# Building the gate table of a product-key retrieval: VectorE's key numbers in PSUM, and half of the second one-hots on VectorE

## The chip, the cores and the metric

The kernel runs on one core of one Trainium2 chip. The metric is device time in microseconds, from one launch that takes all inputs and gives all outputs. The kernel before takes 2154.51 us (median of three runs, 2152.59 to 2160.33). Engines are named as the profile names them: PE is TensorE (PEld its weight loads), DVE is VectorE, ACT is ScalarE, POOL is GpSimd, SP is SyncE, which here only issues DMAs.

## The reference, cut to what matters

One transformer layer on 512 tokens of 1024 channels: a token mixer (dilated and differential attention, gated, projected), then a retrieval over 128 x 128 = 16384 experts of one neuron each, then a last norm. The change touches only the retrieval of the second 256 tokens.

```
# per token and head: 16 best of 128 x 128 product keys, softmax over them
ids   = key1 * 128 + key2              # 8 heads x 16 slots = 128 experts per token
gates = softmax(best_s)
u = u_tab[ids];  act = gelu(einsum('cd,chkd->chk', x, u))
v = v_tab[ids];  out = einsum('chkd,chk->cd', v, gates * act)
```

For a token, the gates can be written as a 128 x 128 table G with G[key2, key1] = sum over the token's 128 slots of gate * (key2 of the slot) one-hot * (key1 of the slot) one-hot. That is a matrix product of two one-hot matrices, with slots as the summed dimension, and it is how the kernel gets the table for the second 256 tokens.

## The kernel before, in words

The tokens go through in two halves of 256. The first half's retrieval is done by rows: for each of its tokens' slots a row of `u_tab`, later of `v_tab`, is gathered (indirect DMA, line 814, issued by POOL) and multiplied or added on DVE (lines 842 and 852); 56 of the `v_tab` rows of one tile are added on PE instead (line 871, with a diagonal matrix that ACT makes in line 868). These rows are "pumped": a few are issued with each piece of the other work, by a table of rates (`RATE`; per four tokens of the gate table 0.45 rows of line 842 and 0.4 of line 871). The places of gathered rows, of raw weights and of those diagonal matrices are one ring of seven.

The second half's retrieval goes over all experts: 64 passes with the whole of `u_tab` and `v_tab` (lines 1102 to 1155, called the sweep below), weighted by the gate table. The gate table is built before the sweep, in a loop over 64 groups of four tokens (line 1157). A group is called a slot of the loop below. One slot is:

- o2, the one-hots of key 2 of four tokens (128 x 512): `iota` holds the key numbers 0 to 127 along the columns, `idT[:, 1]` the chosen keys, a token a column. In every fourth slot (`O3 = 4`) DVE makes it with one comparison (line 1162); in the other 48 slots POOL subtracts (line 1164), and ACT makes a one-hot of the difference with a square and a relu of one minus it (lines 1165 and 1166).
- o1, the one-hots of key 1 times the gates: four comparisons on DVE, one a token, with key and gate as per-partition scalars (line 1168).
- four products on PE into one PSUM bank (line 1172; two bank tiles `s_ps` in turn), and two copies of the bank into the table by ACT (lines 1174 and 1175).
- the pumped rows, issued after the slot's last product.

`iota`, `idT`, o1 and o2 all lie in SBUF. o1 and o2 of a slot are the two halves of one tile `one`; there are four such tiles, two for even and two for odd slots, so a slot's one-hots can't be written before the products of the slot four earlier are done. Before the loop, `idT` is turned round by six transposes on PE (line 1117), each copied back by ACT (line 1118).

The order of the work on each engine is made by the compiler layer's list scheduler from the program order, priorities and its own durations, and each engine works off its list in order. Semaphores carry the dependencies between engines.

Of the kernel before, what the change touches and what calls it, by code (L numbers as in the profile page):

```python
# [11 lines left out]
F32 = mybir.dt.float32  # L12
# [5 lines left out]
ALU = mybir.AluOpType  # L18
# [4 lines left out]
P = 128  # L23
# [13 lines left out]
# rows of the retrieval issued with each weight unit, block or slot of the other work, by stage  # L37
# [17 lines left out]
O3 = 4  # L55
# [30 lines left out]
def block(ctx, tc, x, cT, w_ada, bT, b_row, g1T, norm2_g, w_in, w_pa, w_pb, w_out, lq1, lk1, lq2, lk2,  # L86
# [18 lines left out]
    def shared(nm):  # L105
        """the places of weights and of gathered rows, in turn"""
        return wp.tile([P, D], F32, name=nm, tag="wraw", bufs=7)
# [3 lines left out]
    def place_of(kind, nm, dt=F32):  # L111
        """a unit among the weights' places: raw, high and low parts; a third of the parts only in the front"""
# [8 lines left out]
    def front_place(i):  # L121
        """sixteen units of the front, none of which waits for another's place"""
# [24 lines left out]
    def rsqrt(v, n, nm):  # L147
        """1/sqrt(v), [P, n]"""
# [23 lines left out]
    # ---- small operands  # L172
# [18 lines left out]
    # ---- silu(c)  # L191
# [5 lines left out]
    # ---- modulation: sums over the eight rows of a partition, then over the partitions  # L197
# [24 lines left out]
    def first_modulation(i):  # L222
        """shift and scale of the channels 256 i .. 256 i + 256"""
# [22 lines left out]
    def mod_rows(sec, t):  # L246
        """sections 2..5 of the modulation, a row each in DRAM; the second scale with its norm's weights"""
# [25 lines left out]
    # ---- first norm  # L273
# [63 lines left out]
    # ---- weights in two parts that the one-pass product carries exactly  # L337
    def load_unit(src, nm):
        """src: a [P, a, b] view of DRAM with a b = 1024"""
# [14 lines left out]
    def cols(src, kt, c0, nm):  # L354
        """128 columns, for use as the stationary side"""
# [11 lines left out]
    def cols256(src, kt, c0, nm):  # L367
        """256 columns, for use as the moving side"""
# [4 lines left out]
    def mm3(out_ps, a, b, kt, last=0):  # L373
        """sum over k of a.T @ b, both in two parts; last: the side whose low part is used last"""
# [10 lines left out]
    # ---- relative position bias, as bands  # L385
# [20 lines left out]
    def bias_band(t, h, at, o, m, w):  # L406
        """t[p, at + i w + j] = vec[head, o + i LEN_D + p + j], i < m: rows of a block in reverse"""
# [4 lines left out]
    # ---- lambda  # L412
# [16 lines left out]
    # queries by head: head s of a pair keeps its half of the rows, the other half is zero. The queries of a block  # L429
    # stand in reverse, as the bands do; the transpose of the outputs turns them back.  # L430
# [12 lines left out]
    # ---- keys and values of the first half wait in DRAM for the second  # L443
# [3 lines left out]
    def query(hin, c0, q, nm):  # L447
        """q: [P, 2, HW]"""
# [8 lines left out]
    def key(b, hin, c0, k, i):  # L457
        """k: [P, T]"""
# [24 lines left out]
    # ---- dilated attention: the three groups of a head share one softmax, which is what their merge by  # L483
    # denominators amounts to
# [61 lines left out]
    # ---- differential attention  # L546
    def diff_block(n, q, kk, bd, vb, po, at):
        """one block of queries: q [P, 2, P], keys, bias band, values by block"""
# [23 lines left out]
    def diff_finish(ob, dst, h0):  # L572
        """norm of two heads' outputs, ob: [P, 2, HW], transposed and split into dst"""
# [21 lines left out]
    def mixer(b, between):  # L595
        """attention of half b: both branches' outputs in two parts, channels on partitions"""
# [49 lines left out]
    # ---- the retrieval's choice  # L646
# [8 lines left out]
    def begin_topk(n, t):  # L655
        """t: [P, 768]"""
# [14 lines left out]
    # a pair of ranks (i, j) can be among the best sixteen only if (i + 1)(j + 1) <= 16: row 0 whole, eight of  # L671
    # rows 1..7, one of rows 8..15, in the order of the full table
# [4 lines left out]
    def choose(n, h0, nh, out):  # L677
        """row and column keys of the chosen pairs, heads h0 .. h0 + nh: two [P, 16 nh], a slot a column"""
# [32 lines left out]
        # the keys at those ranks: one of sixteen, small integers that bfloat16 holds exactly  # L711
# [22 lines left out]
    def scores(n, h, qts, held=None):  # L734
        """two tiles, one head: qts: both halves of the queries, [P, HW]"""
# [323 lines left out]

    _, held = tail(0, oa, ob, finish, retrieve)  # L1060

    # ---- second half
    idT = sb.tile([P, 3, 256], F32, name="idT")

    def choose_late(b, g):
# [165 lines left out]
```

## Time and profile before

| what | value |
|---|---|
| median of three runs | 2154.51 us |
| lowest, highest run | 2152.59, 2160.33 us |
| span of the profiled execution | 2148.4 us |
| median of the runs less that span | 6.1 us |
| PE, DVE busy | 1875.4 us (87%), 1839.9 us (86%) |
| POOL, ACT busy | 1257.4 us (59%), 970.7 us (45%) |
| stage of the gate table on DVE | 1209.63 to 1370.28 us |

The profile gives one execution, of which it records the span from the first to the last instruction; what lies around the span is taken as the difference to the median, 6.1 us. Busy time is the union of an engine's records; a record's duration reaches from its start to its end, and on DVE the next record can begin a little (some 0.08 us) before the last one ends, so the pitch from start to start of back-to-back instructions is shorter than the duration. A tuple such as 328/335/3780 is smallest, median and largest duration in ns.

### The profile page before, as it was taken

Reading aid. Unit: us, or ns where it says so; the run is one execution under the profiler, and the core shown is the slowest. Engines: PE = TensorE matmul, PEld = TensorE weight load, DVE = VectorE, ACT = ScalarE, POOL = GpSimd, SP = SyncE. Lnnn points to the kernel's source line nnn. Section 1 sums busy time; section 2 is a strip of 40 time slices with the busy share of each in tenths; the row PEclk is TensorE's granted clock in tenths of the full one; section 3 lists DMA queues with packets and bytes.
Section 4 is the critical chain, followed back from the end, with each engine's and each line's share of the span. In section 5 each row is a group of like instructions: output and inputs, shape, how many; then the busy total and the mean of one; then the engine's idle time right before and its main releaser. Section 6 shows DMA issues by size and latency. Waiting matters only on the chain.

```text
span 2148.4 us, 34562 instructions
## 1 busy us (share of the span) xinstructions
PE 1875.4 (87%) x12324; PEld 1668.1 (78%) x12324; DVE 1839.9 (86%) x3515; ACT 970.7 (45%) x1725; POOL 1257.4 (59%) x797
## 2 busy tenths in 40 slices
PE   6999989887778799878687877889999999999995
PEld 6889889887666687768684455678988889998885
DVE  7757865689999999899889999978999898888777
ACT  2544575442333356543232366534444444444442
POOL 2323323456676676667675766667675665655564
PEclk9999999999999999989798999999999999999998
DMA  9968766758898999889956755788888999998886
GB/s 296 281 198 255 212 178 178 233 175 265 281 313 280 315 325 315 295 291 307 304 186 228 251 169 184 247 284 309 316 316 313 343 346 324 342 335 309 306 308 236
DMA packets 369889, 588.00 MB, mean 274 GB/s; under 512 B 24962, under 2 KB 261002, under 8 KB 369716
## 3 DMA queue, kind: packets, MB, share of 16 engines
q1 hardware_dynamic: 295700, 316.79, 45.3%
q0 software_dynamic: 73728, 268.47, 35.6%
q8 instruction: 97, 1.59, 0.3%
q14 instruction: 76, 0.62, 0.1%
q10 hardware_dynamic: 288, 0.52, 0.1%
HBM read 575.13 MB, written 10.58 MB: 273 GB/s over the span
## 4 chain that ended last, share of the span: by engine, by line
PE 37%; DVE 35%; DMA 14%; issue 8%; POOL 3%; ACT 2%; SPq 1%; POOLq 0%; DVEq 0%; ACTq 0%
PE mm L379 12%; PE acc L1154 9%; PE s_ps L379 9%; DVE grow L842 8%; DMA grow<-in_v_tab_dram,ids 7%; DVE one L1168 3%; DVE wacc L210 2%; DMA wa<-in_w_ada_dram 2%; POOL grow L814 1%; DVE elo L291 1%; DMA grow<-in_u_tab_dram,ids 1%; PE s_ps L1172 1%; DVE rep L666 1%; PE sc L509 1%; DVE acc_rows L852 1%
## 5 line engine op out<-in xcount | busy, mean ns | idle before, releaser
L814 POOL DMA_INDIRECT grow<-in_v_tab_dram,ids x256 | 331.8, 1296 | 300.8 <-DVE ga L852 59.0
L814 POOL DMA_INDIRECT grow<-in_u_tab_dram,ids x256 | 329.6, 1287 | 221.7 <-DVE grow L842 69.8
L842 DVE SCALAR_TENSOR_TENSOR grow<-grow,h 128x1024 f32<-128x1024 f32 x256 | 350.7, 1378 | 6.9 <-DMA grow<-in_u_tab_dram,ids 5.4
L290 ACT CAST ehi<-eraw 128x1024 fp32r<-128x1024 f32 x145 | 152.6, 1053 | 228.7 <-PE acc L1154 75.7
L852 DVE SCALAR_TENSOR_TENSOR ga<-grow,act,ga 128x1024 f32<-128x1024 f32 x127 | 162.8, 1282 | 58.2 <-DMA grow<-in_v_tab_dram,ids 57.6
L290 ACT CAST more<-eraw 128x1024 fp32r<-128x1024 f32 x111 | 116.7, 1051 | 152.7 <-PE acc L1154 62.1
L379 PEld LDWEIGHTS s_ps<-h2T,more 128*128 128x128 f32 x1320 | 166.5, 191 | 4.9 <-ACT more L290 0.2
L1154 PE MATMUL acc<-more,w 128*128 128x512 f32 x672 | 163.4, 392 | 7.3 <-DVE w L291 6.4
L379 PE MATMUL s_ps<-h2T,more 128*128 128x256 f32 x1320 | 168.2, 283 | 0.0
L1154 PE MATMUL acc<-ehi,w 128*128 128x512 f32 x576 | 151.3, 399 | 17.4 <-DVE w L291 14.8
L852 DVE SCALAR_TENSOR_TENSOR acc_rows<-grow,act,acc_rows 128x1024 f32<-128x1024 f32 x71 | 124.4, 1751 | 38.7 <-DMA grow<-in_v_tab_dram,ids 38.2
L1154 PEld LDWEIGHTS acc<-more,w 128*128 128x128 f32 x672 | 127.1, 189 | 34.7 <-DVE w L291 6.8
L379 PE MATMUL s_ps<-h2T,ehi 128*128 128x256 f32 x1168 | 152.0, 283 | 0.0
L379 PEld LDWEIGHTS s_ps<-h2T,ehi 128*128 128x128 f32 x1168 | 145.8, 192 | 0.6
L291 DVE TENSOR_TENSOR elo<-eraw,ehi 128x1024 fp32r<-128x1024 f32 x95 | 136.0, 1432 | 9.4 <-ACT ehi L290 9.2
L1154 PEld LDWEIGHTS acc<-ehi,w 128*128 128x128 f32 x576 | 103.7, 190 | 42.6 <-DVE w L291 21.6
L291 POOL TENSOR_TENSOR elo<-eraw,ehi 128x1024 fp32r<-128x1024 f32 x50 | 123.0, 2459 | 12.6 <-ACT ehi L290 11.8
L1168 DVE TENSOR_SCALAR one<-iota,idT 128x128 f32<-128x128 f32 x256 | 116.5, 534 | 0.3 <-ACT idT L1118 0.3
L379 PE MATMUL mm<-wh_v,h 128*128 128x256 f32 x640 | 102.0, 311 | 15.5 <-ACT wh_v L290 13.1
L1172 PEld LDWEIGHTS s_ps<-one 128*128 128x128 f32 x512 | 69.2, 203 | 54.4 <-ACT G L1175 22.2
L291 DVE TENSOR_TENSOR more<-eraw,more 128x1024 fp32r<-128x1024 f32 x75 | 103.7, 1384 | 6.7 <-ACT more L290 6.5
L871 PE MATMUL ga<-grow,diag 128*128 128x512 f32 x224 | 108.1, 627 | 0.1
(304 smaller groups left out, 4682.5 us busy)
## 6 DMA issues: line engine op xcount, KB each, us to landing
eraw<-in_uT_dram SPq DMA_DIRECT2D x128, 512.0 KB
eraw<-in_v_tab_dram SPq DMA_DIRECT2D x128, 512.0 KB
wa<-in_w_ada_dram SPq DMA_DIRECT2D x48, 512.0 KB
w_v<-in_w_in_dram SPq DMA_DIRECT2D x40, 512.0 KB
w_k<-in_w_in_dram SPq DMA_DIRECT2D x40, 512.0 KB
w_gl<-in_w_in_dram SPq DMA_DIRECT2D x32, 512.0 KB
w_wql<-in_w_q_dram SPq DMA_DIRECT2D x32, 512.0 KB
w_q<-in_w_in_dram SPq DMA_DIRECT2D x24, 512.0 KB
```

Source lines behind the costliest of these rows:

```text
L210: nc.vector.scalar_tensor_tensor(acc, wa[:, k, :], c, acc, op0=ALU.mult, op1=ALU.add)
L290: nc.scalar.copy(hi, src)
L291: (eng or nc.vector).tensor_sub(lo, src, hi.bitcast(F32))
L379: r = nc.tensor.matmul(out_ps, a(i, k), b(j, k), start=(n == 0), stop=(n == 3 * kt - 1))
L509: nc.tensor.matmul(pS[:, at[g] - o:at[g] - o + w[g]], q[g][:, s, n * P:(n + 1) * P], k3[g][:, first[g] * P:(gn + 1) * P], start=True, stop ...
L814: nc.gpsimd.indirect_dma_start(out=r, out_offset=None, in_=tab, in_offset=bass.IndirectOffsetOnAxis(ap=ids[:, s:s + 1], axis=0))
L842: nc.vector.scalar_tensor_tensor(r, r, 1.0, h2, op0=ALU.mult, op1=ALU.mult, accum_out=a)
L852: nc.vector.scalar_tensor_tensor(acc[n], r, a, acc[n], op0=ALU.mult, op1=ALU.add)
L871: nc.tensor.matmul(pe_acc[0][:, sl], dg, r[:, sl], start=(s == 0), stop=(s == NPE - 1), skip_group_check=True)
L1154: nc.tensor.matmul(acc[b][hf], w[i][:, 256 * j + P * b:256 * j + P * b + P], V[jj][:, hf, :], start=(e == 0 and i + jj == 0), stop=(e == N ...
L1168: nc.vector.tensor_scalar(o1[:, t, :], iota, idT[:, 0, t0 + t:t0 + t + 1], idT[:, 2, t0 + t:t0 + t + 1], op0=ALU.is_equal, op1=ALU.mult)
L1172: last = nc.tensor.matmul(pg[:, t * P:(t + 1) * P], o2[:, t, :], o1[:, t, :], start=True, stop=True)
```

## The change

VectorE's comparisons of the table's loop read the key numbers from a PSUM bank. A new pool `pg` holds this bank (`iota_ps`, filled once by ACT before the loop) and three bank tiles `g_ps` for the loop's products, in place of the two tiles that the products shared with the sweep. `O3` goes from 4 to 2, so that DVE makes o2 in every second slot (32 of 64), and POOL and ACT in the others. POOL still reads `iota` from SBUF. The sweep's pool `pp` with `s_ps` and the four accumulators is opened after the loop, when `pg` is given back. The rest of the diff takes out comments and is left out here.

```
-O3 = 4
+O3 = 2
...
-    pp = ctx.enter_context(tc.tile_pool(name="pp", bufs=1, space=PSUM))
+    pg_guard = tc.tile_pool(name="pg", bufs=1, space=PSUM)
+    pg = pg_guard.__enter__()
+
+    def g_ps():
+        return pg.tile([P, 512], F32, name="g_ps", tag="g", bufs=3)
...
-    acc = [[pp.tile([P, 512], F32, name=f"acc{b}{hf}") for hf in range(2)] for b in range(2)]
...
+    iota_ps = pg.tile([P, 512], F32, name="iota_ps")[:, 0:P]
+    nc.scalar.copy(iota_ps, iota)
     for t0 in range(0, 256, 4):
...
-        pair2 = (iota[:, None, :].to_broadcast([P, 4, P]), idT[:, 1, t0:t0 + 4][:, :, None].to_broadcast([P, 4, P]))
+        along = [P, 4, P]
+        key2 = idT[:, 1, t0:t0 + 4][:, :, None].to_broadcast(along)
         if t0 // 4 % O3 == 0:
-            nc.vector.tensor_tensor(o2, *pair2, ALU.is_equal)
+            nc.vector.tensor_tensor(o2, iota_ps[:, None, :].to_broadcast(along), key2, ALU.is_equal)
         else:
-            nc.gpsimd.tensor_tensor(o2, *pair2, ALU.subtract)
+            nc.gpsimd.tensor_tensor(o2, iota[:, None, :].to_broadcast(along), key2, ALU.subtract)
...
-            nc.vector.tensor_scalar(o1[:, t, :], iota, idT[:, 0, t0 + t:t0 + t + 1],
+            nc.vector.tensor_scalar(o1[:, t, :], iota_ps, idT[:, 0, t0 + t:t0 + t + 1],
...
-        pg = s_ps()
+        pt = g_ps()
...
+    pg_guard.__exit__(None, None, None)
+    pp = ctx.enter_context(tc.tile_pool(name="pp", bufs=1, space=PSUM))
+    acc = [[pp.tile([P, 512], F32, name=f"acc{b}{hf}") for hf in range(2)] for b in range(2)]
```

In the changed kernel the comparison for o2 is line 1167, POOL's subtraction 1169, ACT's two activations 1170 and 1171, the comparisons for o1 line 1173, the fill of the bank line 1160, the products 1177 and their copies 1179 and 1180.

How the work stands on DVE at the start of the loop, before (`oh` is scratch of the choice of the last keys, `idT` the chosen keys, `grow` a gathered row):

```order
L719 TENSOR_TENSOR oh<-oh 128x128x8
L1162 TENSOR_TENSOR one<-iota,idT 128x512
L719 TENSOR_TENSOR oh<-oh 128x128x4
L719 TENSOR_TENSOR oh<-oh 128x128x2
L722 TENSOR_TENSOR idT<-oh 128x64 x2
L842 SCALAR_TENSOR_TENSOR grow,act_9338<-grow,h_1_9336 128x1024
L1168 TENSOR_SCALAR one<-iota,idT 128x128 x16
L842 SCALAR_TENSOR_TENSOR grow,act_9338<-grow,h_1_9336 128x1024
L1162 TENSOR_TENSOR one<-iota,idT 128x512
L1168 TENSOR_SCALAR one<-iota,idT 128x128 x8
```

And with the change, at the same place of DVE's list:

```order
L719 TENSOR_TENSOR oh<-oh 128x128x8
L719 TENSOR_TENSOR oh<-oh 128x128x4
L719 TENSOR_TENSOR oh<-oh 128x128x2
L722 TENSOR_TENSOR idT<-oh 128x64 x2
L842 SCALAR_TENSOR_TENSOR grow,act_9338<-grow,h_1_9336 128x1024 x2
L1167 TENSOR_TENSOR one<-iota_ps,idT 128x512
L1173 TENSOR_SCALAR one<-iota_ps,idT 128x128 x8
L1167 TENSOR_TENSOR one<-iota_ps,idT 128x512
L1173 TENSOR_SCALAR one<-iota_ps,idT 128x128 x8
L842 SCALAR_TENSOR_TENSOR grow,act_9338<-grow,h_1_9336 128x1024
```

The first comparison for o2 no longer stands inside the choice of the last keys; two row products stand ahead of the first one-hots, and after that there is one comparison for o2 with every eight for o1.

On ACT at the same place, before (`diag` are the diagonal matrices of line 868, `tp` the bank of the transposes):

```order
L1118 COPY idT<-tp 128x128 x2
L1165 ACTIVATE one<-one 128x512
L1166 ACTIVATE one<-one 128x512
L1165 ACTIVATE one<-one 128x512
L868 ACTIVATE diag<-ident,act_5631 128x128 x8
L1166 ACTIVATE one<-one 128x512
L1165 ACTIVATE one<-one 128x512
L1118 COPY idT<-tp 128x128
L1166 ACTIVATE one<-one 128x512
L1118 COPY idT<-tp 128x128 x3
L1174 COPY G_12228<-s_ps 128x16x4
```

And with the change:

```order
L1118 COPY idT<-tp 128x128 x2
L1170 ACTIVATE one<-one 128x512
L1171 ACTIVATE one<-one 128x512
L1170 ACTIVATE one<-one 128x512
L868 ACTIVATE diag<-ident,act_5631 128x128 x8
L1171 ACTIVATE one<-one 128x512
L1118 COPY idT<-tp 128x128 x4
L1160 COPY iota_ps<-iota 128x128
L1179 COPY G_12228<-g_ps 128x16x4
```

The fill of `iota_ps` (line 1160) stands behind all six copies of `idT`, and two activations of one slot are gone from in front of them.

On POOL, from the first slot on, before:

```order
L814 DMA grow<-in_u_tab_dram,ids_3662 128x1024
L1164 TENSOR_TENSOR one<-iota,idT 128x512 x3
L814 DMA grow<-in_v_tab_dram,ids_3661 128x1024
L814 DMA grow<-in_u_tab_dram,ids_3662 128x1024
L814 DMA grow<-in_v_tab_dram,ids_3661 128x1024
L814 DMA grow<-in_u_tab_dram,ids_3662 128x1024
L814 DMA grow<-in_v_tab_dram,ids_3661 128x1024
L1164 TENSOR_TENSOR one<-iota,idT 128x512 x2
```

And with the change:

```order
L814 DMA grow<-in_u_tab_dram,ids_3662 128x1024
L1169 TENSOR_TENSOR one<-iota,idT 128x512 x2
L814 DMA grow<-in_v_tab_dram,ids_3661 128x1024
L814 DMA grow<-in_u_tab_dram,ids_3662 128x1024
L814 DMA grow<-in_v_tab_dram,ids_3661 128x1024
L814 DMA grow<-in_u_tab_dram,ids_3662 128x1024
L814 DMA grow<-in_v_tab_dram,ids_3661 128x1024
L814 DMA grow<-in_u_tab_dram,ids_3662 128x1024
L1169 TENSOR_TENSOR one<-iota,idT 128x512
```

The gathers are the same; of POOL's runs of two and three subtractions, mostly single ones are left.

## Rows read from the trace of the kernel before

**Rows 1.** The page's first line.

```profile
span 2148.4 us, 34562 instructions
```

**Rows 2.** Busy time by window, for the loop's stage; the first row names the columns.

```profile
core 0: us, PE busy (x) PEld busy (x) DVE busy (x) ACT busy (x) POOL busy (x), PEclk, DMA share, GB/s
1209.63:1370.28 160.65, 122.00 (x604) 85.53 (x603) 160.20 (x334) 101.13 (x249) 110.39 (x102) 0.92 0.58 187
```

**Rows 3.** Groups by line in this window: count, busy us, mean ns, idle before.

```profile
L1168 DVE TENSOR_SCALAR one<-iota,idT 128x128 f32<-128x128 f32 x256 | 116.5, 534 | 0.3 <-ACT idT L1118 0.3
...
L1164 POOL TENSOR_TENSOR one<-iota,idT 128x512 f32<-128x512 f32 x48 | 51.5, 1091 | 8.3 <-PE s_ps L1172 6.2 <-ACT diag L868 1.5
L842 DVE SCALAR_TENSOR_TENSOR grow<-grow,h 128x1024 f32<-128x1024 f32 x28 | 33.7, 1212 | 0.0
...
L814 POOL DMA_INDIRECT grow<-in_u_tab_dram,ids x28 | 31.5, 1127 | 23.4 <-DVE grow L842 10.7 <-DVE one L1168 9.1 <-PE s_ps L1172 1.7
L1165 ACT ACTIVATE one<-one 128x512 f32<-128x512 f32 x48 | 29.8, 628 | 35.7 <-POOL one L1164 35.7
...
L1162 DVE TENSOR_TENSOR one<-iota,idT 128x512 f32<-128x512 f32 x16 | 14.8, 924 | 0.0
```

**Rows 4.** Timeline, 1231 to 1239 us: start, duration, instructions merged.

```profile
1231.12 4.55 DVE L1168 TENSOR_SCALAR one<-iota,idT 128x128 f32<-128x128 f32 x4
...
1232.04 3.03 POOL L1164 TENSOR_TENSOR one<-iota,idT 128x512 f32<-128x512 f32 x3
...
1236.74 2.14 DVE L1168 TENSOR_SCALAR one<-iota,idT 128x128 f32<-128x128 f32 x8
```

**Rows 5.** Timeline at the start of the loop, 1209 to 1219 us.

```profile
1209.63 3.78 DVE L1162 TENSOR_TENSOR one<-iota,idT 128x512 f32<-128x512 f32 x1
...
1209.82 3.04 POOL L1164 TENSOR_TENSOR one<-iota,idT 128x512 f32<-128x512 f32 x3
...
1216.00 0.24 ACT L1118 COPY idT<-tp 128x128 f32<-128x128 f32 x1
...
1216.28 4.28 DVE L1168 TENSOR_SCALAR one<-iota,idT 128x128 f32<-128x128 f32 x16 [0.33 <-ACT idT L1118]
...
1218.46 0.27 ACT L1118 COPY idT<-tp 128x128 f32<-128x128 f32 x1 [0.56 <-PE tp L1117]
```

**Rows 6.** Single lines on DVE: count, smallest/median/largest ns, first and last start.

```profile
L1168 DVE TENSOR_SCALAR one<-iota,idT x256: 328/335/3780, 1216.3 to 1370.0; 128x128 f32<-128x128 f32 x128
...
L1162 DVE TENSOR_TENSOR one<-iota,idT x16: 676/678/3779, 1209.6 to 1362.3; 128x512 f32<-128x512 f32 x16
...
L979 DVE TENSOR_SCALAR h_k<-tp,m2T x8: 531/542/547, 432.5 to 1080.3; 128x256 f32<-128x256 f32 x8
...
L954 DVE TENSOR_TENSOR ot<-mm,mod x16: 408/416/425, 404.6 to 1060.8; 128x256 f32<-128x256 f32 x16
...
L955 DVE TENSOR_TENSOR x<-x,ot x16: 408/458/3037, 408.5 to 1062.4; 128x256 f32<-128x256 f32 x16
...
L791 DVE TENSOR_TENSOR grow<-grow,acc x4: 671/680/680, 2132.1 to 2136.6; 128x512 f32<-128x512 f32 x4
```

**Rows 7.** Timeline of the second norm's transposes, in both halves: reads from PSUM.

```profile
434.97 0.54 DVE L979 TENSOR_SCALAR h_k<-tp,m2T 128x256 f32<-128x256 f32 x1
435.43 0.53 DVE L979 TENSOR_SCALAR h_k<-sc,m2T 128x256 f32<-128x256 f32 x1
...
1074.38 0.73 POOL L980 TENSOR_TENSOR h2T<-h_k,h2T 128x256 fp32r<-128x256 f32 x1 [1.49 <-DVE h_k L979]
...
1074.61 0.55 DVE L979 TENSOR_SCALAR h_k<-sc,m2T 128x256 f32<-128x256 f32 x1 [0.31 <-ACT h2T L978]
```

**Rows 8.** Timeline of PE in the loop, 1227 to 1231 us.

```profile
1227.00 1.88 PE L871 MATMUL ga<-grow,diag 128*128 128x512 f32 x4
...
1228.71 1.95 PE L1172 MATMUL s_ps<-one 128*128 128x128 f32 x16
```

**Rows 9.** The page's group of row sums in the sweep, and what ended DVE's idle time before them.

```profile
L852 DVE SCALAR_TENSOR_TENSOR ga<-grow,act,ga 128x1024 f32<-128x1024 f32 x127 | 162.8, 1282 | 58.2 <-DMA grow<-in_v_tab_dram,ids 57.6
```

More of the change, by code (lines that the diff above doesn't have):

```diff
@@ L1167, in block @@
         for t in range(4):
-            nc.vector.tensor_scalar(o1[:, t, :], iota, idT[:, 0, t0 + t:t0 + t + 1],
+            nc.vector.tensor_scalar(o1[:, t, :], iota_ps, idT[:, 0, t0 + t:t0 + t + 1],
                                     idT[:, 2, t0 + t:t0 + t + 1], op0=ALU.is_equal, op1=ALU.mult)
-        pg = s_ps()
+        pt = g_ps()
         for t in range(4):
-            last = nc.tensor.matmul(pg[:, t * P:(t + 1) * P], o2[:, t, :], o1[:, t, :], start=True, stop=True)
-        pv = pg.rearrange("p (t i) -> p i t", t=4)
+            last = nc.tensor.matmul(pt[:, t * P:(t + 1) * P], o2[:, t, :], o1[:, t, :], start=True, stop=True)
+        pv = pt.rearrange("p (t i) -> p i t", t=4)
         nc.scalar.copy(G0[:, :, t0:t0 + 4], pv[:, 0:2 * EARLY, :])
```

## The prediction

> **What bounds the kernel now.** I read the page first, for the span [rows 1], then the busy time by window around the loop that builds the gate table, since only that loop is edited. The reader should see one thing there: of the 160.65 us from 1209.63 to 1370.28, DVE is busy 160.20, while PE has 122.00, POOL 110.39 and ACT 101.13 [rows 2]. DVE never waits in this stage, everybody else does. So the stage lasts as long as DVE's list, and the question is what that list is made of.
>
> The groups by line answer it [rows 3]. The 256 comparisons of line 1168 hold DVE for 116.5 us, with a mean of 534 ns, but their median is 335 ns and their largest 3780 [rows 6]. The timeline shows both kinds side by side: eight of them in 2.14 us where POOL makes no one-hots, and four of them in 4.55 us where POOL makes three in a row for 3.03 us [rows 4]. The same happens to line 1162: 678 ns in the median, but 3.78 us at 1209.63, with three of POOL's subtractions from 1209.82 on [rows 5, 6]. DVE's busy time is thus partly waiting inside instructions, and no view of idle time shows it.
>
> How much: undisturbed, the eight start (2.14 - 0.335) / 7 = 0.258 us apart, so 256 need 66.0 us; measured 116.5, which leaves 50.5 us of stall. The 16 of line 1162 start about 0.60 us apart (678 ns less the 0.08 us by which DVE's records overlap: 0.335 against 0.258), 9.6 us; measured 14.8, another 5.2. Together some 56 us, against 51.5 us in which POOL runs line 1164 at all [rows 3]: nearly every microsecond of POOL's subtractions is taken from DVE.
>
> **The change part by part.** *Key numbers in PSUM, line 1173.* The trace has the same instruction with a PSUM source at twice the width: line 979, two per-partition scalars, 256 columns, 531 to 547 ns [rows 6]; two in a row start 435.43 - 434.97 = 0.46 us apart [rows 7]. The width costs (678 - 408) / 256 = 1.05 ns a column (lines 1162 and 954's smallest, 512 and 256 columns) [rows 6], so 128 columns take 0.13 us less: 0.32 us a piece, 256 of them 82 us. From both sides: not under the 0.25 us that the SBUF form of the same width needs (64 us), not over the 0.46 us of the wider one (118 us). I take 0.32, since width is all that differs from line 979.
>
> Do these instructions still stall? Line 979 at 1074.61 started 0.23 us into a subtraction of POOL's and took 0.55 us, as always [rows 7]. Line 954, which reads PSUM and SBUF, never took over 425 ns in 16; line 955 right behind it, the same width with both sources in SBUF, took up to 3037 [rows 6]. I take no stall for lines 1167 and 1173.
>
> [...]
>
> *Half of o2 on DVE, line 1167.* 32 instead of 16, one source in PSUM, 512 columns: line 791's 671 to 680 ns, so 0.60 us in the row, 19.2 us. POOL loses 16 subtractions (16 x 1.09 = 17.5 us) and ACT 32 activations (32 x 0.63 = 20 us) [rows 3]; both wait for others today, so this by itself shortens nothing.
>
> *Row products, line 842.* The same 28, 1.21 us each, 1.14 us apart: 32 us. Both sources lie in SBUF, as with line 955, so these can still stall on POOL. Today they don't, because the comparison in front has waited already. With 32 subtractions of 1.05 us in a stage of some 140 us, one is under way a quarter of the time: 28 / 4 = 7 cases of half an instruction or a little more, 4 us. Bounds: none, and 28 whole ones, 29 us; I take 4.
>
> *The start.* Today the first comparisons of line 1168 start at 1216.28, when the third of six copies of `idT` is back; DVE worked ahead while the other transposes ran until 1218.46 + 0.27 [rows 5]. Now the fill of the bank stands behind all six copies and the first one-hot behind that: about 1218.7, less half a microsecond that two activations gone from ACT's list give, plus some 0.3 for the copy; I take 1218.6. Until then DVE has the rest of the key choice (1.4 us), which now meets POOL's first two subtractions, and two row products (2.3 us), so that some 5 us of the first 9.0 are stalled or idle. Queued behind are all of DVE's one-hots, and nothing else needs DVE there.
>
> *The sum for the stage.* 9.0 to the first one-hot, 82 + 19.2 for the comparisons, 26 row products 29.6, their stalls 4, and 2 us for places where DVE will now have to wait for PE or POOL: 146 us. Before 160.65, so 14.5 us less; at the end of the loop the new pool makes the sweep's first bank wait for the last two copies of ACT, 0.5 us. That leaves 14. Cover: PE's own work in the stage is 64 slots of 0.98 us (16 records, two slots, in 1.95) and 28 rows of 1.88 us [rows 8], 115 us; POOL's 110.39 less 17.5, 93; ACT's about 81. All are under 146, so DVE remains the longest.
>
> The sweep behind starts that much earlier and its work is the same. The span goes from 2148.4 to 2134.4; with the 6.1 us that lie around it (median 2154.5 less the span) the forecast is 2140.5.
>
> **The rivals.** *More than that.* If the row products never meet POOL and DVE never waits, the stage is 140 us and with a short start (DVE's one-hots 2 to 3 us earlier) 137: 23 us less, 2131. For: DVE's records have no idle today. Against: the row products have two SBUF sources.
>
> *The gain is partly lost.* The sweep's row sums wait 57.6 us for gathers on DVE [rows 9]; a shifted order of gathers and row sums there could give back some of the gain, or the waits in the loop come to 8 us and not 2. Gain 5 on the middle: 2149.5. For: the scheduler reorders DVE's and POOL's lists in the sweep too. Against: the same gathers stand in the sweep, and DMA is busy only 0.58 in the loop.
>
> *A fee for narrow reads from PSUM.* If 128 columns cost more than the line through 256 and 512 says, halfway to the bound of 0.46 us, 0.39, line 1173 takes 17 us more: gain gone, 3 us over, 2157.5. [...] Against it are the rows at 256 and 512 columns; no row shows 128.
>
> *Slower: the ring of four `one` tiles.* DVE can't write a slot's one-hots before PE is through with the slot four earlier. In an odd slot that hangs on POOL (a gather 1.13, the subtraction 1.09), ACT (two times 0.63), PE (a row 1.88 and the slot's 0.98): 6.3 us in a row [rows 3, 8]. DVE needs (82 + 19 + 32) / 64 = 2.1 us a slot, 8.3 for four, so the loop is covered by 2 us. It decides from 8.3 on; over 10 us (a second and third gather in front of the subtraction, and each waiting for a row product) it takes the stage past today's. At 10.8 us a round, 16 rounds are 173 us: 12 more than before, 2166.5. For: POOL's gathers do wait for DVE's row products (10.7 us) and ACT for POOL (35.7) [rows 3]. Against: today's DVE meets the same ring with 48 such slots and doesn't wait once. The same side holds that the change doesn't do what it says, because comparisons from PSUM stall on POOL after all: 32 subtractions at 1.05 are 33 us more, 2170 or so; line 954 speaks against it.
>
> **How the numbers follow.** Forecast, a gain of 9 to 20 us: 0.56. More: 0.10. Partly lost: 0.17. Fee: 0.10. Slower by the ring or the lasting stalls: 0.07. A measurement of this kernel tells a difference from none from about 0.5% on, 10.8 us: under 2143.7 is faster, over 2165.3 slower. Of the forecast 0.50 lies under 2143.7, with the first rival 0.60 faster; the rest of it, the partly lost and the fee 0.33 the same; 0.07 slower. The range from 2127 to 2156 leaves out a little of the first rival, half of the fee and the slower cases.
>
> **What would show it.** In the changed profile: line 1173 with median near 400 ns and a largest not far above; line 1167 at 680 and never 3000; the stage from the choice's end to the last comparison at 146 us; line 842 there with some of 1.5 to 2.3 us; DVE idle before the first line 1167, waiting for ACT's line 1160, and idle little after. The forecast is wrong if line 1173's median is over 450 ns, if DVE's idle time in front of lines 1167 and 1173 comes to over 10 us, or if the loop shrinks as said and the end doesn't move with it.

## The result, and the profile after

The changed kernel takes 2126.47 us (median of four runs, 2122.78 to 2128.08) against 2155.12 (2152.59 to 2160.33): a ratio of 0.9865, 95% interval 0.9833 to 0.9896. That is 28.6 us less where 14 were forecast, and half a microsecond under the range. Two later measurements gave 2131.32 against 2150.57 and 2123.17 against 2146.49, 19 and 23 us less, gains that the range would have held. The direction and the way the loop is bound came out as forecast; the step on the sweep behind it did not.

The span of the profiled execution (its time is 2122.78, so 1.8 us lie around it), against [rows 1]:

```profile
span 2121.0 us, 34486 instructions
```

The loop's stage by window, from DVE's first fold of the last key choice (line 719, the same place of its list at which [rows 2] starts) to the last comparison, columns as there. It is 16.6 us shorter. DVE is busy 137.71 of 144.07 us, and its idle 6.3 us all stand ahead of the first one-hot (below); POOL, ACT and PE keep their slack:

```profile
1205.90:1349.97 144.07, 116.45 (x615) 84.80 (x613) 137.71 (x348) 86.95 (x221) 92.02 (x86) 0.95 0.66 208
```

The groups by line there, against [rows 3]. L1173 (L1168 before) fell from 116.5 to 84.8 us although each undisturbed instruction became longer; twice as many L1167 cost only 21.7; L842 rose by 3.3:

```profile
L1173 DVE TENSOR_SCALAR one<-iota_ps,idT 128x128 f32<-128x128 f32 x256 | 84.8, 396 | 0.0
L842 DVE SCALAR_TENSOR_TENSOR grow<-grow,h 128x1024 f32<-128x1024 f32 x28 | 37.0, 1331 | 6.3 <-DMA grow<-in_u_tab_dram,ids 4.7 <-issue 1.5
L1167 DVE TENSOR_TENSOR one<-iota_ps,idT 128x512 f32<-128x512 f32 x32 | 21.7, 677 | 0.0
...
L1169 POOL TENSOR_TENSOR one<-iota,idT 128x512 f32<-128x512 f32 x32 | 35.6, 1115 | 14.7 <-PE g_ps L1177 13.5 <-ACT one L1170 0.7
```

The single lines (smallest/median/largest ns) show why, against [rows 6]: 335 became 396 ns in the median, but 3780 became 402 at the most. What still stalls is L842, with both sources in SBUF: its largest is 2086, and 37.0 less 28 times 1.211 leaves 3.1 us, of which 0.9 fall on the one behind the last comparison. POOL tells the two kinds apart: as the profile draws its records, 50 of the changed kernel's 288 comparisons begin and end inside one of POOL's subtractions, and the longest of these takes 682 ns; in the kernel before none of 272 does, and all 35 that take over 0.8 us overlap a subtraction.

```profile
L1173 DVE TENSOR_SCALAR one<-iota_ps,idT x256: 392/396/402, 1218.6 to 1349.6; 128x128 f32<-128x128 f32 x128
...
L1167 DVE TENSOR_TENSOR one<-iota_ps,idT x32: 671/676/684, 1218.0 to 1345.6; 128x512 f32<-128x512 f32 x32
...
L842 DVE SCALAR_TENSOR_TENSOR grow<-grow,h x28: 1205/1211/2086, 1210.9 to 1349.9; 128x1024 f32<-128x1024 f32 x28
```

The timeline at the loop's start on DVE (start, duration), against [rows 5]. The key choice's L719 now meets POOL and takes 3.55 us for three, then DVE waits 1.55 us for nothing that the profile names and 4.71 us for a gathered row. The last row is eight comparisons in 2.63 us, so a pitch of (2.63 - 0.396) / 7 = 0.319 us:

```profile
1205.31 3.55 DVE L719 TENSOR_TENSOR oh<-oh 128x1024 bf16<-128x1024 bf16 x3
...
1210.90 1.23 DVE L842 SCALAR_TENSOR_TENSOR grow<-grow,h 128x1024 f32<-128x1024 f32 x1 [1.55 <-issue]
...
1216.84 1.22 DVE L842 SCALAR_TENSOR_TENSOR grow<-grow,h 128x1024 f32<-128x1024 f32 x1 [4.71 <-DMA grow<-in_u_tab_dram,ids]
...
1217.99 0.68 DVE L1167 TENSOR_TENSOR one<-iota_ps,idT 128x512 f32<-128x512 f32 x1
1218.60 2.63 DVE L1173 TENSOR_SCALAR one<-iota_ps,idT 128x128 f32<-128x128 f32 x8
```

Where 27.4 us of span went. The marks are the starts of the last line 713 (the key choice's last comparison), of PE's last product of the loop and of PE's last product of all, read to some 0.2 us here and below:

| stretch | before | changed | difference |
|---|---|---|---|
| up to the last line 713 | 1205.4 | 1201.7 | -3.7 |
| from there to PE's last product of the loop | 167.0 | 148.6 | -18.4 |
| sweep, to PE's last product | 761.1 | 754.8 | -6.3 |
| rest | 14.9 | 15.9 | +1.0 |

The sweep by window, first of the kernel before, then of the changed one. PE is busy 729.03 and 730.53 us, the same work; what differs is the time in which PE is not busy, 32.1 and 24.3 us:

```profile
1372.40:2133.50 761.10, 729.03 (x4609) 657.64 (x4608) 642.31 (x520) 336.30 (x389) 476.39 (x283) 0.99 0.88 317
```

```profile
1350.30:2105.10 754.80, 730.53 (x4609) 660.61 (x4609) 661.56 (x522) 336.88 (x388) 478.78 (x284) 0.99 0.90 321
```

The waits in the sweep (total us, times, longest), before:

```profile
DVE ga L852 <- DMA grow<-in_v_tab_dram,ids: 57.6, 41, 3.4
DVE acc_rows L852 <- DMA grow<-in_v_tab_dram,ids: 38.2, 21, 6.1
...
PE acc L1154 <- DVE w L291: 21.2, 17, 6.4
```

and changed:

```profile
DVE ga L852 <- DMA grow<-in_v_tab_dram,ids: 44.7, 36, 3.1
DVE acc_rows L852 <- DMA grow<-in_v_tab_dram,ids: 28.3, 22, 4.1
...
PE acc L1156 <- DVE w L291: 13.6, 10, 5.8
```

How the one becomes the other is seen in the timeline of the kernel before near its end. The split of the last weights (`w`, L291) stands on DVE's list behind three row sums, each of which waits for its gathered row; PE can't go on without `w` and stands 6.36 us:

```profile
2120.07 1.29 DVE L852 SCALAR_TENSOR_TENSOR ga<-grow,act,ga 128x1024 f32<-128x1024 f32 x1 [0.83 <-DMA grow<-in_v_tab_dram,ids]
2121.64 1.29 DVE L852 SCALAR_TENSOR_TENSOR ga<-grow,act,ga 128x1024 f32<-128x1024 f32 x1 [0.28 <-DMA grow<-in_v_tab_dram,ids]
2125.62 1.29 DVE L852 SCALAR_TENSOR_TENSOR ga<-grow,act,ga 128x1024 f32<-128x1024 f32 x1 [2.69 <-DMA grow<-in_v_tab_dram,ids]
2126.82 0.68 DVE L291 TENSOR_TENSOR w<-wg,w 128x512 fp32r<-128x512 f32 x1
...
2127.55 2.08 PE L1154 MATMUL acc<-more,w 128*128 128x512 f32 x4 [6.36 <-DVE w L291]
```

### The profile page after: what moved, and what is told of

It reads as the page before. It is cut to its first block, busy times and chain, and to the rows that moved or that the text cites. A ratio compares the mean times of both kernels' runs of the same rounds, so it can differ in the third digit from the quotient of the medians.

```text
span 2121.0 us, 34486 instructions
## 1 busy us (share of the span) xinstructions
PE 1867.4 (88%) x12324; PEld 1665.5 (79%) x12324; DVE 1840.3 (87%) x3531; ACT 955.5 (45%) x1694; POOL 1243.6 (59%) x781
## 4 chain that ended last, share of the span: by engine, by line
PE 38%; DVE 30%; DMA 11%; issue 8%; POOL 4%; ACT 2%; POOLq 0%; DVEq 0%; SPq 0%; ACTq 0%
PE mm L379 11%; PE acc L1156 11%; PE s_ps L379 10%; DVE grow L842 9%; DMA grow<-in_v_tab_dram,ids 5%; DVE one L1173 3%; PE ga L871 2%; DMA grow<-in_u_tab_dram,ids 2%; POOL grow L814 2%; POOL elo L291 1%; DMA wa<-in_w_ada_dram 1%; DVE wl_k L291 1%; PE ops L533 1%; DVE wacc L210 1%; DVE one L1167 1%
## 5 line engine op out<-in xcount | busy, mean ns | idle before, releaser
L842 DVE SCALAR_TENSOR_TENSOR grow<-grow,h 128x1024 f32<-128x1024 f32 x256 | 359.0, 1411 | 12.8 <-DMA grow<-in_u_tab_dram,ids 9.5
L852 DVE SCALAR_TENSOR_TENSOR acc_rows<-grow,act,acc_rows 128x1024 f32<-128x1024 f32 x71 | 119.3, 1681 | 29.8 <-DMA grow<-in_v_tab_dram,ids 28.3
L291 DVE TENSOR_TENSOR elo<-eraw,ehi 128x1024 fp32r<-128x1024 f32 x95 | 138.1, 1454 | 7.8 <-ACT ehi L290 7.0
L291 POOL TENSOR_TENSOR elo<-eraw,ehi 128x1024 fp32r<-128x1024 f32 x50 | 127.6, 2552 | 6.8 <-ACT ehi L290 3.6
L291 DVE TENSOR_TENSOR more<-eraw,more 128x1024 fp32r<-128x1024 f32 x75 | 107.8, 1439 | 5.2 <-ACT more L290 5.1
L871 PE MATMUL ga<-grow,diag 128*128 128x512 f32 x224 | 102.8, 601 | 0.2 <-DMA grow<-in_v_tab_dram,ids 0.2
L379 PEld LDWEIGHTS mm<-wh_v,h 128*128 128x128 f32 x640 | 90.6, 211 | 14.7 <-ACT wh_v L290 9.7
L379 PE MATMUL mm<-h,wh_k 128*128 128x256 f32 x640 | 96.1, 302 | 6.5 <-ACT qz L454 5.4
```

What stands on the lines that cost most here:

```text
L291: (eng or nc.vector).tensor_sub(lo, src, hi.bitcast(F32))
L379: r = nc.tensor.matmul(out_ps, a(i, k), b(j, k), start=(n == 0), stop=(n == 3 * kt - 1))
L842: nc.vector.scalar_tensor_tensor(r, r, 1.0, h2, op0=ALU.mult, op1=ALU.mult, accum_out=a)
L852: nc.vector.scalar_tensor_tensor(acc[n], r, a, acc[n], op0=ALU.mult, op1=ALU.add)
L871: nc.tensor.matmul(pe_acc[0][:, sl], dg, r[:, sl], start=(s == 0), stop=(s == NPE - 1), skip_group_check=True)
```

## The experiments

Theory A: what goes beyond the loop is spread from run to run. Theory B: it is the order of the sweep's lists, which the change alters by the way (aligned as well as can be, 17% of DVE's list there stands in another order). Theory C, a later rival: the changed loop shortens the sweep behind it whatever its order.

**Both kernels again, and the parts of the change.** `c0_before` and `c1_after` are the two kernels. `e1_psum` has the key numbers in PSUM and the three banks alone, `e2_half` only the other `O3`, `e3_banks` only the pool of three banks, without the bank of key numbers:

```
e1_psum:  -O3 = 2          (against the changed kernel)
          +O3 = 4
e2_half:  -O3 = 4          (against the kernel before)
          +O3 = 2
e3_banks: -nc.vector.tensor_scalar(o1[:, t, :], iota_ps, ...   (against e1_psum; so too for o2)
          +nc.vector.tensor_scalar(o1[:, t, :], iota, ...
```

> The kernel before, run again for a second profile. The loop's stage (start of the first key-choice fold on DVE to the end of the last one-hot or row product) was 161 us before and 147 us after, as forecast (146); but the span fell by 27, not 14: 3.7 us were gone ahead of the loop, where both kernels have the same lists, and 9 behind it, most of it in the last quarter of the sweep. Theory A (chance from run to run): the stretch ahead of the loop and the sweep differ from the first profile by several us here too. Theory B (the lists behind the loop are in another order and the sweep gains by it): the sweep from the first to the last weighting on DVE is 735 us again, within 2; only the stretch ahead may wander.

> The changed kernel, run again. Theory A (chance): the sweep from the first to the last weighting, 725 us in the first profile of it, comes out some us longer, toward 735, and the median gain on five rounds lies nearer to 15 to 20 us. Theory B (order of the lists): the sweep is 725 again within 2, and the gain again 27 to 29 us. Both: the loop's stage 147 us, comparisons from PSUM at 396 ns with none over 450.

> Only the key numbers in PSUM and the three banks; VectorE makes o2 in every fourth slot as before. By DVE's sum the stage is 9 to the first one-hot, 256 x 0.32 = 82, 16 x 0.60 = 9.6, 26 row products 29.6 and some 6 for their meetings with 48 subtractions of POOL: 137 us, 10 less than the changed kernel, if DVE remains the longest. Rival (the ring of four one-hot tiles, through POOL and ACT in three slots of four): DVE now waits in front of its comparisons, 10 us or more in all, and the stage is no shorter than 147.

> Only the half of o2 on VectorE; key numbers in SBUF, two banks as before. If POOL's subtractions hold up every DVE comparison from SBUF for as long as they run: 256 x 0.258 = 66, 32 x 0.60 = 19.2, 28 row products 32, POOL's 32 x 1.05 = 34 as stalls, some 6 at the start: 157 us for the stage, 4 less than before, single comparisons up to 1.8 us or more. Rival (the stalls are due to something else, such as the buffers, and would not shrink with POOL's count): 170 us, since 16 more of DVE's o2 come on top.

`c0_before`: one run, 2160.62 us; loop to PE's mark 167.0, sweep 767.1. `c1_after`: 2131.32, ratio 0.991 (0.9883 to 0.9936); loop 149.6, sweep 756.9. A third profile of the changed kernel gave 149.2 and 754.2. The loop is thus the same to a microsecond. Part of what A wanted came: the gain fell to 19.3 (15 to 20 by A, 27 to 29 by B), and the sweep of the kernel before was 6 us longer the second time, where B wanted 2 at most. But the changed sweep (754.8, 756.9, 754.2) lies under before's (761.1, 767.1) in every profile, so A does not carry all of the sweep's part. It does carry the front, which lay between 1200 and 1214 us in all profiles of this study.

`e1_psum`: 2138.52, ratio 0.9947 (0.9924 to 0.997); loop 146.6, sweep 764.7. `e2_half`: 2146.73, ratio 0.9974 (0.9953 to 0.9996); loop 165.3, sweep 765.8. The first part shortens the loop even more than the whole, though by 2 us and not the 10 that were expected: with 48 subtractions its row products are held up more (42.7 us, 8.8 over 28 times 1.211, where the changed kernel has 3.1). The second part alone shortens the loop by 1.7 us, not by 4, because its comparisons still meet POOL. The groups by line of `e2_half` in the loop's window, one-hots in SBUF, show it: a mean of 458 where its median is 334, 862 where its median is 680.

```profile
L1168 DVE TENSOR_SCALAR one<-iota,idT 128x128 f32<-128x128 f32 x256 | 98.0, 458 | 0.0
...
L1162 DVE TENSOR_TENSOR one<-iota,idT 128x512 f32<-128x512 f32 x32 | 27.5, 862 | 0.0
```

But `e1_psum`, with the shorter loop, was slower than the changed kernel by 7 us: its sweep was the longer one. That points to B.

> The kernel before with the loop's pool of three banks alone: key numbers in SBUF, a quarter of the o2 on VectorE. In the loop VectorE's list is the same and never waited for a bank, so: loop 176 to 178 us, the comparisons' stalls as before (mean of the per-token comparisons 0.50 to 0.54 us). Theory A: the sweep 760 to 772, the median within 8 us of the kernel before. Theory B: the sweep's lists are those of a new layout; its length may lie anywhere from 756 to 775, and the median follows it, up to 10 us either way, with the loop unchanged.

`e3_banks`: 2152.21, ratio 1.0007 (0.9987 to 1.0027); loop 169.0, comparisons 503 ns in the mean, sweep 762.0. The third bank alone gives nothing.

The traces hold the orders themselves. In the sweep DVE's lists of `e1_psum`, `e2_half` and `e3_banks` are 95 to 97% those of the kernel before, and like it they have sweeps of 762 to 767 us, whatever their loops are. The changed kernel's list is 84% that of before, and of all kernels at this rate only it has sweeps of 757 us or less.

**The sweep fenced off.** The whole sweep is put behind the loop's last copy, so that the scheduler lays it out alike for both loops: DVE's sweep lists are then 99% alike in order instead of 84%, and 94% alike to that of the kernel before without a fence; PE's are identical.

```
+    last_copy = nc.scalar.copy(G1[:, :, t0:t0 + 4], pv[:, 2 * EARLY:, :])
...
+    with tc.issue_after(last_copy.ins):
         w = s_part(0)
         for ep in range(N_TILES // 2):
...
```

> The kernel before, with the whole sweep put behind the loop's last copy out of a bank, so that the scheduler lays out the sweep without regard to how the loop went. Theory A (the gain beyond the loop's own is the spread of the front and the sweep from run to run): the loop as before, 178 us from the last comparison of the key choice to the first weighting; the sweep 760 to 772 us, as in the kernels run so far; a time within 10 us of the kernel before. Theory B (the order of the sweep's lists, which the change alters by the way, is worth the rest): the sweep now has nearly the order of the changed kernel with the same fence, so its length is the same as there within 3 us, whatever that length is. What is compared is this run with the next one.

> The changed kernel with the same fence before the sweep. Its lists from the fence on differ from those of the fenced kernel before in 7 places on VectorE, 1 on GpSimd and 1 on ScalarE, against 65, 11 and 24 without fences. Both theories: the loop 163 us, 15 less than the fenced kernel before. Theory B (order of the sweep's lists): the sweep is as long as in the fenced kernel before within 3 us, so the median is lower by the loop's 15 us, 12 to 18, and no more. Theory A (spread of the front and the sweep): the same median gain, but single profiles whose sweeps differ by up to 6 us either way. A third, C (the changed loop hands the sweep a better state, gathers or rows further ahead, whatever the order): the gain is 20 to 28 us and the sweep is 5 to 12 us shorter than in the fenced kernel before.

`f1_before_fenced`: 2162.83, ratio 1.0057 (1.0036 to 1.0078). `f2_after_fenced`: 2142.59, 0.9963 (0.9946 to 0.998). Each is 11 to 19 us slower than the same kernel without the fence, with loops of 167.2 and 150.9: the fence, which changes the order and none of the work, moves the end that far. But the pair's gain is 20.2, not 12 to 18; the sweeps still differ, 775.1 and 770.0. By itself this favours C over B, so other orders were needed. It is weak, though: the two profiles of the kernel before, with identical lists, differ by 6.0. And with a list near that of before, the changed kernel's sweep is no longer short, 770.0 where it was 754 to 757, as B has it.

**Other orders: the rate of rows in the sweep.** `RATE["c"]` says how many rows are issued with a block of the sweep; `g1` and `g2` have 0.70, `g3` and `g4` 0.82, with the fence; `h1` to `h3` have no fence.

```
-        "c": 0.76}
+        "c": 0.70}      (0.82, 0.88)
```

> The fenced kernel before with another rate of rows in the sweep (0.70 a block instead of 0.76), which gives VectorE's and GpSimd's lists there another order (53% and 47% of it as with 0.76... the rest moved) and leaves front and loop alone. Theory B (the sweep's order sets some ten microseconds): the sweep, from the loop's last product on TensorE to the last product of all, lies anywhere from 755 to 785 us, unlike the 775 at the rate 0.76. Theory A (spread from run to run): 765 to 778. Compared pairwise with the next run.

> The fenced changed kernel with the rate 0.70; VectorE's list in the sweep is 95% that of the run before, GpSimd's 99%. Theory B: the gain against the run before is what the loop ends earlier on TensorE, 16 us (14 to 18), and the sweep as long as there within 3 us. Theory C (the changed loop makes the sweep behind it shorter, whatever its order): the gain is 20 us or more, as the fenced pair at 0.76 gave.

> The fenced kernel before with the rate 0.82: a third order of the sweep. Theory B: the sweep 755 to 785 us, unlike the other two orders by some 5 to 15 us. Theory A: 765 to 778.

> The fenced changed kernel with the rate 0.82; VectorE's list in the sweep is 97% that of the run before. Theory B: 14 to 18 us less than the run before. Theory C: 20 us or more. If this pair and the one at 0.70 fall on the two sides of 16, the 20 of the pair at 0.76 was what the seven differing places of its lists are worth.

> The kernel before with the sweep's rate at 0.82, no fence. With the fence the rate took 22 us off (2162.8 to 2140.7); without it the sweep was 12 us shorter at 0.76, so part of that is had already. Theory B (the sweep's order and the place of its rows): rows end before the last expert pairs, the sweep is 750 to 758 us from the loop's last product to the last of all, against 761 and 767, and the median 2138 to 2146.

> The changed kernel with the rate 0.82, no fence; VectorE's list in the sweep is 95% that of the run before. Theory B: the median is 14 to 18 us under the run before, so 2121 to 2131, and the sweeps are equal within 3 us. Theory C (the changed loop shortens the sweep): 20 us or more under it, 2115 to 2122. As a version: better than the changed kernel if the median is under 2121.

> The changed kernel with the rate 0.88, no fence. If the sweep at 0.82 is already bound by TensorE (756 us of which some 715 are its own products), more rows per block in its first half only make the low halves of the expert tables later: the same within 5 us as at 0.82, or slower by up to 10.

| sweep | median, loop as before | median, changed loop | gain | loop to PE's mark | sweep on PE |
|---|---|---|---|---|---|
| 0.76, no fence | 2155.12, 2150.57, 2146.49 | 2126.47, 2131.32, 2123.17 | 28.6, 19.3, 23.3 | 167.0 / 148.6 | 761.1, 767.1 / 754.8, 756.9, 754.2 |
| 0.76, fence | 2162.83 | 2142.59 | 20.2 | 167.2 / 150.9 | 775.1 / 770.0 |
| 0.70, fence | 2244.59 | 2221.28 | 23.3 | 166.3 / 149.2 | 839.1 / 842.3 |
| 0.82, fence | 2140.73 | 2127.20 | 13.5 | 165.1 / 149.4 | 756.0 / 757.2 |
| 0.82, no fence | 2138.93 | 2122.21 | 16.7 | 166.7 / 148.7 | 750.0 / 746.9 |

The loop gives 15.7 to 18.4 us in every row. Where the sweep covers its rows, at 0.82, and DVE's lists in it are 95 to 97% alike, the pairs gain 13.5 and 16.7 us: the loop and no more. Each of these gains is uncertain by some 5 us, judged by the spread of its runs; the two together lie under the 20 that C wanted in every order, and C falls there. At 0.70 the sizes were missed by far: both kernels became 70 to 95 us slower than the unfenced kernel before, not 755 to 785 for the sweep but 840. With that the gain of 23.3 there, from runs that spread over 25 us, decides little; its profiled sweeps go the other way by 3 us. At 0.88 the median was 2136.70 (0.9928; 0.9899 to 0.9957), 14 us slower than at 0.82 where 10 at the most were expected: PE waits 12.9 us, 2.1 at 0.82, for the low halves that POOL makes of the expert table. Two profiles show the mechanism. Waits in the sweep of `g1_before_c70`:

```profile
DVE ga L852 <- DMA grow<-in_v_tab_dram,ids: 157.7, 59, 6.3
DVE acc_rows L852 <- DMA grow<-in_v_tab_dram,ids: 88.5, 38, 5.6
...
PE acc L1154 <- DVE w L291: 67.2, 28, 8.1
```

and of `h1_before_c82`, the old loop:

```profile
DVE acc_rows L852 <- DMA grow<-in_v_tab_dram,ids: 20.4, 16, 4.6
DVE ga L852 <- DMA grow<-in_v_tab_dram,ids: 9.4, 7, 2.5
PE acc L1154 <- DVE w L291: 5.7, 6, 1.5
```

PE's waits for `w` follow the row sums' waits for gathers, 67.2 (with the fence), 21.2 and 5.7 us at three rates. The row sums' last instruction says why. Count, durations, first and last start in `h1_before_c82`, the row sums and then the weightings:

```profile
L852 DVE SCALAR_TENSOR_TENSOR ga<-grow,act,ga x127: 1273/1277/1291, 1642.4 to 2088.1; 128x1024 f32<-128x1024 f32 x127
...
L1141 DVE TENSOR_TENSOR wg<-wg,G x64: 675/689/3168, 1383.1 to 2112.5; 128x512 f32<-128x512 f32 x64
```

Here the rows are through 24 us before the last weighting (2088.1, 2112.5). In the kernel before they end after it (2128.3, 2118.6), at 0.70 with 2232.1 and 2202.9, so that gathers, DVE and PE meet in the last pairs, and there a different order is worth microseconds. The changed loop hands on no head start that could do this instead: at its end 198 row sums are left, 197 before, and 314 of the 512 gathers are issued, 315 before.

**The parts again, with the sweep out of the way.** `k1_psum_c82` is `e1_psum` at 0.82, `k2_after_c82` the changed kernel at 0.82, `k3_after_c76` the changed kernel.

> Key numbers in PSUM and the three banks, a quarter of the o2 on VectorE as before, the sweep's rate 0.82. Theory B (the sweep's order made the difference between the first part and the whole change): the loop ends on TensorE some 2 us earlier than in the changed kernel, as at 0.76, so the median is that of the run k2 within 4 us. Rival: the second part is worth 5 us or more of its own, since GpSimd and ScalarE, relieved, hand the sweep a better start: k2 is 5 to 10 us faster than this.

> The changed kernel at the rate 0.82 again: 2117 to 2127, as before on another chip.

> The changed kernel itself. If the rate 0.82 is better for it, this is 3 to 9 us above k2 (2131.3 and 2122.2 on two chips); if its own order in the sweep is as good as that at 0.82, the same within 3 us (2126.5 in the first measurement).

2121.80 (0.9882; 0.9859 to 0.9904), 2120.43 (0.9872; 0.9851 to 0.9892) and 2123.17 (0.9883; 0.9862 to 0.9904). The first part of the change is as fast as the whole, with the loop 146.6 against 149.3 us, to the 6 or so us that these runs tell apart. So nothing shows that its second part adds, and the 7 us between `e1_psum` and the changed kernel were most likely the sweep's order. The profile of `k1_psum_c82` doesn't help: it is of that kernel's slowest run, 2135.79 us, with a sweep of 761.6 us against 750.2 in `k2_after_c82`. And 0.82 doesn't beat the changed kernel: 2.7 us, less than these runs tell apart.

**A shorter list for DVE.** `e6_gate` lets ACT multiply the gates into o2 in POOL's slots, so that DVE makes o1 there with one comparison of 512 columns instead of four of 128 (`ngate` holds the gates with their sign turned):

```
+            for t in range(4):
+                g = idT[:, 2, t0 + t:t0 + t + 1]
+                nc.scalar.activation(o2[:, t, :], o2[:, t, :], AF.Relu, bias=g, scale=ngate[:, t0 + t:t0 + t + 1])
...
+            nc.vector.tensor_tensor(o1, iota_ps[:, None, :].to_broadcast(along), key1, ALU.is_equal)
```

> The changed kernel with the gates of the slots in which GpSimd and ScalarE make o2 multiplied into o2 by ScalarE (four activations of 128 columns with the gate as bias and its negative as scale, in place of one of 512), so that VectorE makes o1 there with one comparison of 512 columns from the bank in place of four of 128. VectorE saves 32 times (4 x 0.32 - 0.60) = 22 us of its list. If VectorE still sets the loop: 163 - 22 = 141 us, and a median of 2131 - 22 = 2109. Rival: the ring of four one tiles now binds, since ScalarE needs some 0.6 to 1 us more for each such slot and its chain goes from 6.3 to about 7.2 us, while VectorE needs 1.75 us a slot, 7.0 for four: then the loop is 148 to 158 us, with VectorE idle before the comparisons for want of a one tile, and the median 2115 to 2127.

2152.21, ratio 1.0 (0.9978 to 1.0021): both expectations missed. The groups of DVE from 1230 to 1362 us, in its loop:

```profile
L1178 DVE TENSOR_SCALAR one<-iota_ps,idT 128x128 f32<-128x128 f32 x128 | 43.2, 395 | 0.0
L842 DVE SCALAR_TENSOR_TENSOR grow<-grow,h 128x1024 f32<-128x1024 f32 x27 | 40.2, 1490 | 11.8 <-DMA grow<-in_u_tab_dram,ids 11.8
L1182 DVE TENSOR_TENSOR one<-iota_ps,idT 128x512 f32<-128x512 f32 x32 | 21.6, 677 | 0.2 <-PE g_ps L1185 0.2
```

The comparisons are as short as meant (43.2 + 21.6 in place of 84.8), but DVE's list isn't the bound any more: row products wait 11.8 us for gathers, which POOL issues from the same list as its subtractions, and these wait 17.6 us for PE to be through with a `one` tile (13.5 in the changed kernel). L842's mean rises to 1490 ns. From the first one-hot on DVE is done 4.4 us sooner than in the changed kernel, but its first one-hot comes 2.4 us later, and PE's last product 6.5 us behind DVE's last comparison, after a wait of 2.57 us for ACT's four activations (line 1175). The loop is 153.1 us, 4.5 longer than the changed kernel's, and the sweep, in yet another order, 768.4.

## Where the prediction was wrong, and what it had right

*What bounds the loop* was right: DVE's list with stalls inside its instructions, and it still sets the stage. The stall was counted somewhat too high: it set busy times against distances of starts. By starts alone the lines 1168 and 1162 fill 113.3 and 13.6 us of the loop before, 47.3 and 4.0 over the undisturbed 66.0 and 9.6, so 51 us and not 56, which is just POOL's 51.5 us of subtractions.

*Line 1173 at 0.32 us without stalls*: 0.319, and 402 ns at the most. `e1_psum` has it alone, 390/395/403. *Line 1167 at 0.60*: 19.2 us for 32, so 0.60, and none above 684 ns. *Row products with 4 us of stalls*: 3.1. *2 us of waits in the loop*: none behind the first one-hot.

*The fee for narrow reads* from PSUM did not come. The rival's 0.39 was an estimate, halfway between 0.32 and the 0.46 of line 979; the measured pitch at 128 columns is 0.319 us. That is 0.061 us over the pitch from SBUF (0.258), but the 0.32 held this already, since line 979, from which it was worked out, reads PSUM itself. At 512 columns the comparison took 676 ns in the median from PSUM (line 1167) and 678 from SBUF (line 1162). No run shows what sets the 0.061, nor why it is missing there.

*The start*: the first one-hot came 12.1 us after the stage's start, not 9.0, and not for the reason given. The fill of the bank (line 1160) started at 1214.5 us and took 0.27, but the second row product ahead of the one-hots waited for its gathered row until 1216.84. The sum for the stage, forecast 146 us, came to 144.1: 12.1 to the first one-hot, and by the distances of starts 81.8 and 19.2 for comparisons and 31.0 for the 25 row products ahead of the last comparison, stalls included.

*The end of the loop* was mis-sized by 2 us. PE's last product started 1.9 us behind the end of DVE's last comparison before and 0.3 behind it now, while the forecast had only a cost of 0.5 there: PE's first product of the sweep does wait for ACT's last copy, 0.74 us. So the loop gave 18.4 where 14.5 less 0.5 was forecast.

*"The sweep behind starts that much earlier and its work is the same"* is the step that failed. Its work is the same, its length isn't: between the profiles it is 4 to 13 us shorter (761.1 and 767.1 against 754.2 to 756.9). In the first two profiles PE stands 7.8 us less in it, and its waits for `w`, which comes on DVE's list behind row sums that wait for their gathers, fall by 7.6 (21.2 and 13.6). What the runs leave as the cause is the order in which the scheduler laid row sums among weights: kernels with the order of before have its sweep, whatever their loop is. The rival "partly lost" named this very place, the gathers and row sums in a shifted order, but only as a loss; it should have been a term with both signs, of some 10 us. The runs at 0.82, with gains of 13.5 and 16.7, show what the forecast had right once the order is taken out.

*The 6.1 us around the span* are 1.8 by the changed kernel's profiled execution; the other 4.3 are how far, with the same 1.8, the execution profiled before lay under the median. That does no harm to the forecast, which is the median before less 14, but it shows how little one span fixes the end. Between the two spans 27.4 us went, 13.4 more than forecast: 4.4 of the loop, 5.3 of sweep and rest, and 3.7 of the front's spread, which is chance. The changed profile lay 3.7 us under its own median, so 0.6 more come from the two executions' places, and the sum is the 14.0 between 2140.5 and 2126.5.

*The faster rival* is the nearest by its number, 23 us less. Its mechanism did not come: row products met POOL, DVE waited 6.3 us ahead of its one-hots, and the stage took 144 us, not 137.

*The slower rivals*: the ring of four tiles did not bind (no wait of DVE for PE in the loop), though `e6_gate` suggests that it is close behind: with a shorter list for DVE, POOL waits for it. Comparisons from PSUM did not stall (402 and 684 ns at the most).

Left open: which of the places where DVE's sweep lists differ gives the 4 to 13 us, and how much of that is spread between executions, which alone moved one sweep by 6. Single moves in the list weren't tried.

## What to carry to other kernels

Where DVE's instruction is long in the mean and short in the median (534 and 335 ns here), look for POOL at the same moment; here a source in PSUM cost 18% per undisturbed instruction (396 for 335 ns) and the 256 of them still took 84.8 us in place of 116.5. When a change makes a scheduler lay out a later stage anew, give that stage a term of its own with both signs, sized by its waits, and find it by running the pair under another order: where both kernels' later stages are relieved, only the edit is left. And end a filler's work before the stage that it fills: row sums that outlived the last pairs cost the kernel before 11 us (2149.61 and 2138.93, on one chip), the changed kernel no more than these runs tell apart (2.7), and the fenced kernel before 82 with the rate lowered from 0.76 to 0.70.

## What the runs showed of the hardware

- A per-token comparison of 128 columns took 396 ns in the median from PSUM and 335 from SBUF (pitch 0.319 and 0.258 us); a comparison of 512 columns with one source in PSUM took 676, from SBUF 678.
- Beside POOL's chains the SBUF forms took up to 3780 and 3779 ns in the kernel before. The PSUM forms took 403 and 686 ns at the most in the changed kernel's first profile, `c1_after` and `e1_psum`, and 50 of them ran wholly inside a subtraction of POOL's in the changed kernel's first profile, none over 682.
- The front, with the same list on DVE in every kernel of this study, ended between 1200.4 and 1214.4 us over several chips, and between 1201.4 and 1214.4 on one of them: 13 us of spread with nothing changed.
